# Which eighth of which channel a partition holds: s*16+k in the place of k*8+s

## The chip, the cores and the metric

The kernel runs on one core of a Trainium2 chip. A core has five engines that work side by side: TensorE (PE, with its weight loads as PEld), VectorE (DVE), ScalarE (ACT), GpSimd (POOL) and SyncE (SP), and 16 DMA engines that carry data between the memory of the chip (HBM) and the core's own memory (SBUF, 128 partitions). SP, ACT and POOL issue the transfers; each has its own queue. The metric is the device time of one execution in microseconds.

## The reference

The input x has 4 x 8 x 16 = 512 channels of 256 x 256 float32 values (256 KB each, 134 MB in all). Each channel is normalized by itself and scaled by its gamma:

```python
mu = x.mean(axis=(3, 4), keepdims=True)
var = ((x - mu) ** 2).mean(axis=(3, 4), keepdims=True)
x_norm = (x - mu) / np.sqrt(var + 1e-5)
out = x_norm * gamma[None, :, :, None, None]
```

Every value is read once and written once: 268 MB of traffic for two sums, one subtraction and one product a value.

## The kernel before, in words

The channels are worked in 32 units (U) of 16 channels (K). A channel is cut into S = 8 pieces of F = 8192 values (32 KB), so that the 16 x 8 = 128 pieces of a unit fill a tile of 128 partitions, 4 MB. In the kernel before, the view xv reads a unit as (p f): partition p holds the p-th 32 KB of the unit, so partition k*8+s holds piece s of channel k, and a unit is one unbroken stretch of HBM. The view ov does the same for the output.

There are AHEAD = 6 tiles (slots xt0 to xt5), each used in place for load, arithmetic and store. Six loads (line 48) are issued at the start, units 1 and 3 on ACT's queue and the others on SP's. Behind its two loads ACT gets 60 nops. POOL first issues two small transfers: a "touch" of the output with zeros (line 54, 16 rows of 512 B, later overwritten) and the load of gamma into one row (line 55). Then POOL makes constants, among them the matrix navg (lines 66 to 75): a memset to -1/65536 and two affine_selects that put zeros wherever the row and the column belong to different channels. As the partitions of one channel lie side by side, it is a matrix of 8x8 blocks on the diagonal. The gamma row is copied (line 83) into g_rep with 8 copies of each value, and 8 small matmuls turn that into g_col, one column of gammas a partition for each of the NG = 8 groups of channels.

The loop over units then does, for each:

- DVE sums each partition (line 107), while ACT sums its squares (line 108); both go to st.
- PE multiplies st by navg (line 116): each partition gets the sums of its whole channel, negated and divided by the number of values, as ps.
- DVE forms the negated variance (line 117), ACT its root (line 121), DVE the reciprocal (line 125) and the product with gamma (line 127).
- DVE applies mean and scale to the tile in place (line 130).
- ACT issues the store (line 134); SP issues the load of unit u+6 into the same slot, which waits for that store to end.

The order of the instructions on each engine is the program's own (a manual schedule); the queues are worked in order, SP's with loads and ACT's with stores behind its own arithmetic.

Of the kernel before, what the change touches and what calls it, by code (L numbers as in the profile page):

```python
# [1 line left out]

# [4 lines left out]

F32 = mybir.dt.float32
U8 = mybir.dt.uint8
ALU = mybir.AluOpType  # L10
ACTF = mybir.ActivationFunctionType
AX = mybir.AxisListType


@with_exitstack
def kernel(
    ctx: ExitStack,
    tc: tile.TileContext,
    x: bass.AP,
    gamma: bass.AP,  # L20
    out: bass.AP,
):
    nc = tc.nc
    B, G, C, H, W = x.shape
    P = nc.NUM_PARTITIONS
    HW = H * W
    n_ch = B * G * C
    S = 8
    K = P // S
    F = HW // S  # L30
    U = n_ch // K
    NG = (G * C) // K
    AHEAD = 6
    assert HW % S == 0 and (G * C) % K == 0

    xv = x.rearrange("b g c h w -> (b g c h w)").rearrange("(u p f) -> u p f", p=P, f=F)
    ov = out.rearrange("b g c h w -> (b g c h w)").rearrange("(u p f) -> u p f", p=P, f=F)
    gv = gamma.rearrange("g c -> (g c)")

    data = ctx.enter_context(tc.tile_pool(name="data", bufs=1))  # L40
    singles = ctx.enter_context(tc.tile_pool(name="singles", bufs=1))
    psum = ctx.enter_context(tc.tile_pool(name="psum", bufs=4, space=bass.MemoryType.PSUM))
    ctx.enter_context(tc.manual_schedule())

    slots = [data.tile([P, F], F32, name=f"xt{i}") for i in range(AHEAD)]

    def load(u, queue):
        queue.dma_start(out=slots[u % AHEAD][:], in_=xv[u])  # L48


    g_row = singles.tile([1, G * C], F32, name="g_row")
    touch = singles.tile([16, 128], F32, name="touch")
    nc.vector.memset(touch[:], 0.0)  # L53
    nc.gpsimd.dma_start(out=ov[0][0::S, 0:128], in_=touch[:])  # L54
    nc.gpsimd.dma_start(out=g_row[:], in_=gv[None, :])  # L55
    for u in range(AHEAD):
        load(u, nc.scalar if u in (1, 3) else nc.sync)

    for _ in range(60):
        nc.scalar.nop()  # L60

    eps_t = singles.tile([P, 1], F32, name="eps_t")
    nc.gpsimd.memset(eps_t[:], 1e-5)
    one = singles.tile([1, 1], F32, name="one")
    nc.gpsimd.memset(one[:], 1.0)
    navg = singles.tile([P, K, S], F32, name="navg")
    nc.gpsimd.memset(navg[:], -1.0 / HW)  # L67
    nc.gpsimd.affine_select(  # L68
        out=navg[:], in_=navg[:], pattern=[[-S, K], [0, S]], compare_op=ALU.is_ge,
        fill=0.0, base=0, channel_multiplier=1,  # L70
    )
    nc.gpsimd.affine_select(  # L72
        out=navg[:], in_=navg[:], pattern=[[S, K], [0, S]], compare_op=ALU.is_ge,
        fill=0.0, base=S - 1, channel_multiplier=-1,
    )
    navg_w = navg[:].rearrange("p k s -> p (k s)")
    root_eps = singles.tile([P, 1], F32, name="root_eps")
    nc.scalar.activation(out=root_eps[:], in_=eps_t[:], func=ACTF.Sqrt)  # L78
    g_rep = singles.tile([1, NG, K, S], F32, name="g_rep")
    g_ps = psum.tile([P, NG], F32, name="g_ps", bufs=1)  # L80
    g_col = singles.tile([P, NG], F32, name="g_col")

    nc.vector.tensor_copy(  # L83
        out=g_rep[:],
        in_=g_row[:].rearrange("o (n k) -> o n k", n=NG).unsqueeze(3).to_broadcast([1, NG, K, S]),
    )
    for n in range(NG):
        nc.tensor.matmul(  # L88
            out=g_ps[:, n : n + 1],
            lhsT=g_rep[:, n].rearrange("o k s -> o (k s)"),  # L90
            rhs=one[:],
            start=True, stop=True,
        )
    nc.vector.tensor_copy(out=g_col[:], in_=g_ps[:])  # L94

    junk = singles.tile([P, F], U8, name="junk")

    st = singles.tile([P, U, 2], F32, name="st")
    nvar = singles.tile([P, U], F32, name="nvar")
    std = singles.tile([P, U], F32, name="std")  # L100
    rstd = singles.tile([P, U], F32, name="rstd")
    scale = singles.tile([P, U], F32, name="scale")

    squares = []
    for u in range(U):
        t = slots[u % AHEAD]
        nc.vector.reduce_sum(out=st[:, u, 0:1], in_=t[:], axis=AX.X)  # L107
        square = nc.scalar.activation(  # L108
            out=junk[:], in_=t[:], func=ACTF.Square, accum_out=st[:, u, 1:2],
        )  # L110
        if u:

            tc.declare_no_dep(square.ins, squares[-1].ins, reason="junk, ordered by the root between")
        squares.append(square)
        ps = psum.tile([P, 2], F32, name="ps")
        nc.tensor.matmul(out=ps[:], lhsT=navg_w, rhs=st[:, u], start=True, stop=True)  # L116
        nc.vector.tensor_scalar(  # L117
            out=nvar[:, u : u + 1], in0=ps[:, 0:1], scalar1=ps[:, 0:1],
            scalar2=ps[:, 1:2], op0=ALU.mult, op1=ALU.add,
        )  # L120
        nc.scalar.activation(  # L121
            out=std[:, u : u + 1], in_=nvar[:, u : u + 1], func=ACTF.Sqrt,
            bias=eps_t[:], scale=-1.0,
        )
        nc.vector.reciprocal(out=rstd[:, u : u + 1], in_=std[:, u : u + 1])  # L125
        g = u % NG
        nc.vector.tensor_mul(  # L127
            out=scale[:, u : u + 1], in0=rstd[:, u : u + 1], in1=g_col[:, g : g + 1],
        )
        nc.vector.tensor_scalar(  # L130
            out=t[:], in0=t[:], scalar1=ps[:, 0:1], scalar2=scale[:, u : u + 1],
            op0=ALU.add, op1=ALU.mult,
        )
        nc.scalar.dma_start(out=ov[u], in_=t[:])
        if u + AHEAD < U:
            load(u + AHEAD, nc.sync)


# [1 line left out]
_INS = ['x', 'gamma']  # L140
_OUTS = [((4, 8, 16, 256, 256), 'float32')]


# [23 lines left out]
```

## Time and profile before

| What | Value |
|---|---|
| median of 3 runs | 626.86 us (626.76 to 626.90) |
| span of the profiled execution | 624.9 us (the page gives no other time of it) |
| bytes moved | 268.46 MB, 430 GB/s over the span |
| DVE busy | 443.4 us (71%) |
| ACT busy | 238.8 us (38%) |
| PE busy | 21.4 us (3%) |
| POOL busy | 2.4 us |
| sum of a tile (line 107, DVE) | 8.69 us, 32 times |
| squares of a tile (line 108, ACT) | 7.03 us, 32 times |
| scaling of a tile (line 130, DVE) | 4.55 us, 32 times |
| store, issue to landing | median 62.5 us |
| load on SP, issue to landing | median 38.5 us |

A profile page shows one execution. Its slices cut the span in 40 equal parts: the DMA digits are tenths of the 16 DMA engines' time, and GB/s is what they moved. A DMA queue is listed with its packets, bytes and share of 16 engines' time: q1 is SP's, q10 ACT's, q0 POOL's. The chain follows the last instruction back to what released it, step by step. A wait names the waiting engine, its line and what ended the wait. A window gives the busy time of every engine in one stretch of the span.

### The profile page before, as it was taken

What the parts mean: (1) busy time and instruction counts of PE and PEld (TensorE: products, weight loads), DVE (VectorE), ACT (ScalarE), POOL (GpSimd) and SP (SyncE); (2) the same over time, 40 slices, a digit from 0 to 9 for tenths busy, and PEclk for the clock granted to TensorE, in tenths of its full rate; (3) what the DMA queues carried; (4) which work ended last, traced back from release to release, by engine and by line L of the source; (5) the groups of instructions that cost most, each with busy time, mean ns of one, the idle gap of its engine ahead of it and who ended that gap; (6) DMA issues with size and microseconds to landing.
All of it is one profiled execution on the core that took longest, in us unless ns stands there. A gap on an engine that the chain in (4) does not pass through costs nothing.

```text
span 624.9 us, 631 instructions
## 1 busy us (share of the span) xinstructions
PE 21.4 (3%) x80; PEld 19.5 (3%) x80; DVE 443.4 (71%) x163; ACT 238.8 (38%) x98; POOL 2.4 (0%) x11
## 2 busy tenths in 40 slices
PE   0200000000000000000000000000000000000000
PEld 0200000000000000000000000000000000000000
DVE  0588999999776687666786767867668676687730
ACT  0444444444443234432344423444224442244400
POOL 1000000000000000000000000000000000000000
DMA  8999999999999999999999999999999999999998
GB/s 370 436 426 430 422 434 436 436 436 437 432 424 433 436 436 424 436 436 434 436 436 432 422 436 436 434 426 436 436 434 436 436 434 419 436 436 434 426 436 369
DMA packets 9282, 268.46 MB, mean 430 GB/s; under 512 B 1072, under 2 KB 1088, under 8 KB 1088
## 3 DMA queue, kind: packets, MB, share of 16 engines
q10 hardware_dynamic: 4896, 142.61, 52.9%
q1 hardware_dynamic: 4320, 125.83, 46.8%
q0 software_dynamic: 64, 0.01, 0.0%
q14 instruction: 2, 0.02, 0.0%
HBM read 134.22 MB, written 134.23 MB: 430 GB/s over the span
## 4 chain that ended last, share of the span: by engine, by line
another core or an unknown queue 61%; DMA 17%; DVE 15%; SPq 1%; PE 1%; issue 0%; ACT 0%
DVE st L107 10%; DMA xt<-in_x_dram 10%; DMA out_dram<-xt 8%; DVE xt L130 5%; SPq L48 1%; PE ps L116 1%; ACT std L121 0%; DVE nvar L117 0%; DVE rstd L125 0%; DVE scale L127 0%
## 5 line engine op out<-in xcount | busy, mean ns | idle before, releaser
L107 DVE TENSOR_REDUCE st<-xt 128x1 f32<-128x8192 f32 x32 | 277.9, 8685 | 100.4 <-DMA xt<-in_x_dram 100.4
L108 ACT ACTIVATE junk<-xt 128x8192 uint8<-128x8192 f32 x32 | 225.0, 7030 | 275.1 <-DMA xt<-in_x_dram 231.9
L130 DVE TENSOR_SCALAR xt<-xt,ps,scale 128x8192 f32<-128x8192 f32 x32 | 145.6, 4550 | 1.2
L121 ACT ACTIVATE std<-nvar,eps_t 128x1 f32<-128x1 f32 x32 | 9.4, 294 | 79.6 <-DVE nvar L117 79.6
L116 PE MATMUL ps<-st,navg 128*128 128x2 f32 x64 | 17.9, 349 | 557.1 <-DVE st L107 557.1
L116 PEld LDWEIGHTS ps<-st,navg 128*128 128x128 f32 x64 | 16.0, 311 | 558.9 <-issue 558.9
L117 DVE TENSOR_SCALAR nvar<-ps 128x1 f32<-128x1 f32 x32 | 9.2, 287 | 23.8 <-PE ps L116 23.8
L125 DVE RECIPROCAL rstd<-std 128x1 f32<-128x1 f32 x32 | 5.2, 164 | 11.6 <-ACT std L121 11.6
L83 DVE COPY g_rep<-g_row 1x1024 f32<-1x1024 f32 x1 | 0.7, 681 | 14.3 <-DMA g_row<-in_gamma_dram 14.3
L108 ACT ACTIVATION_READ_ACCUMULATOR junk<-xt 128x1 f32 x32 | 6.0, 186 | 0.0
L127 DVE TENSOR_TENSOR scale<-rstd,g_col 128x1 f32<-128x1 f32 x32 | 5.1, 159 | 1.1
L88 PE MATMUL g_ps<-one,g_rep 1*128 1x1 f32 x16 | 3.5, 347 | 16.1 <-DVE g_rep L83 16.1
L88 PEld LDWEIGHTS g_ps<-one,g_rep 1*128 1x128 f32 x16 | 3.5, 325 | 16.1 <-issue 16.1
L94 DVE COPY g_col<-g_ps 128x8 f32<-128x8 f32 x1 | 0.2, 166 | 3.7 <-PE g_ps L88 3.7
L78 ACT ACT_TABLE_LOAD x1 | 1.3, 1283 | 1.7 <-PEq L151 1.7
L53 DVE MEMSET touch<- 16x128 f32 x1 | 0.2, 165 | 0.9 <-PEq L151 0.9
L54 POOL DMA_DIRECT2D out_dram<-touch x1 | 0.6, 619 | 0.8 <-DVE touch L53 0.8
L55 POOL DMA_DIRECT2D g_row<-in_gamma_dram x1 | 0.5, 487 | 0.0
L68 POOL TENSOR_SCALAR_AFFINE_SELECT navg<-navg 128x128 f32<-128x128 f32 x1 | 0.4, 400 | 0.1
L72 POOL TENSOR_SCALAR_AFFINE_SELECT navg<-navg 128x128 f32<-128x128 f32 x1 | 0.4, 399 | 0.1
L67 POOL MEMSET navg<- 128x128 f32 x1 | 0.2, 232 | 0.0
L78 ACT ACTIVATE root_eps<-eps_t 128x1 f32<-128x1 f32 x1 | 0.2, 203 | 0.0
(6 smaller groups left out, 0.6 us busy)
## 6 DMA issues: line engine op xcount, KB each, us to landing
out_dram<-xt ACTq DMA_DIRECT2D x32, 4096.0 KB, 62.5
xt<-in_x_dram SPq DMA_DIRECT2D x30, 4096.0 KB, 38.5
xt<-in_x_dram ACTq DMA_DIRECT2D x2, 4096.0 KB, 31.5
out_dram<-touch POOLq DMA_DIRECT2D x1, 8.0 KB, 9.1
g_row<-in_gamma_dram POOLq DMA_DIRECT2D x1, 0.5 KB, 13.3
```

The lines of the kernel that those rows point to most:

```text
L48: queue.dma_start(out=slots[u % AHEAD][:], in_=xv[u])
L78: nc.scalar.activation(out=root_eps[:], in_=eps_t[:], func=ACTF.Sqrt)
L83: nc.vector.tensor_copy(out=g_rep[:], in_=g_row[:].rearrange("o (n k) -> o n k", n=NG).unsqueeze(3).to_broadcast([1, NG, K, S]),)
L88: nc.tensor.matmul(out=g_ps[:, n : n + 1], lhsT=g_rep[:, n].rearrange("o k s -> o (k s)"), rhs=one[:], start=True, stop=True,)
L107: nc.vector.reduce_sum(out=st[:, u, 0:1], in_=t[:], axis=AX.X)
L108: square = nc.scalar.activation(out=junk[:], in_=t[:], func=ACTF.Square, accum_out=st[:, u, 1:2],)
L116: nc.tensor.matmul(out=ps[:], lhsT=navg_w, rhs=st[:, u], start=True, stop=True)
L117: nc.vector.tensor_scalar(out=nvar[:, u : u + 1], in0=ps[:, 0:1], scalar1=ps[:, 0:1], scalar2=ps[:, 1:2], op0=ALU.mult, op1=ALU.add,)
L121: nc.scalar.activation(out=std[:, u : u + 1], in_=nvar[:, u : u + 1], func=ACTF.Sqrt, bias=eps_t[:], scale=-1.0,)
L125: nc.vector.reciprocal(out=rstd[:, u : u + 1], in_=std[:, u : u + 1])
L127: nc.vector.tensor_mul(out=scale[:, u : u + 1], in0=rstd[:, u : u + 1], in1=g_col[:, g : g + 1],)
L130: nc.vector.tensor_scalar(out=t[:], in0=t[:], scalar1=ps[:, 0:1], scalar2=scale[:, u : u + 1], op0=ALU.add, op1=ALU.mult,)
```

## The change

The views xv and ov cut a unit as (k s f) and walk it as s, then k, then f: partition s*16+k now holds piece s of channel k. In HBM, neighbouring partitions lie 256 KB apart, and each is a row of 32 KB. The number of transfers, their bytes and the queues that issue them are the same. What follows from the new order of partitions is changed with it: the averaging matrix has its non-zero values where row and column differ by a multiple of 16, and is made by a memset to 0 and 15 affine_selects, one for each such diagonal; g_rep repeats the 16 gammas of a group 8 times as a whole instead of each of them 8 times. The touch names the same bytes by the new view. The 60 nops on ACT are gone.

```diff
-    xv = x.rearrange("b g c h w -> (b g c h w)").rearrange("(u p f) -> u p f", p=P, f=F)
-    ov = out.rearrange("b g c h w -> (b g c h w)").rearrange("(u p f) -> u p f", p=P, f=F)
+    xv = x.rearrange("b g c h w -> (b g c h w)").rearrange("(u k s f) -> u s k f", k=K, s=S, f=F)
+    ov = out.rearrange("b g c h w -> (b g c h w)").rearrange("(u k s f) -> u s k f", k=K, s=S, f=F)
...
-    nc.gpsimd.dma_start(out=ov[0][0::S, 0:128], in_=touch[:])
+    nc.gpsimd.dma_start(out=ov[0][0, :, 0:128], in_=touch[:])
...
-    for _ in range(60):
-        nc.scalar.nop()
...
-    navg = singles.tile([P, K, S], F32, name="navg")
-    nc.gpsimd.memset(navg[:], -1.0 / HW)
-    nc.gpsimd.affine_select(
-        out=navg[:], in_=navg[:], pattern=[[-S, K], [0, S]], compare_op=ALU.is_ge,
-        fill=0.0, base=0, channel_multiplier=1,
-    )
-    nc.gpsimd.affine_select(
-        out=navg[:], in_=navg[:], pattern=[[S, K], [0, S]], compare_op=ALU.is_ge,
-        fill=0.0, base=S - 1, channel_multiplier=-1,
-    )
-    navg_w = navg[:].rearrange("p k s -> p (k s)")
+    navg_w = singles.tile([P, P], F32, name="navg")
+    nc.gpsimd.memset(navg_w[:], 0.0)
+    for m in range(-(S - 1), S):
+        nc.gpsimd.affine_select(
+            out=navg_w[:], in_=navg_w[:], pattern=[[-1, P]], compare_op=ALU.not_equal,
+            fill=-1.0 / HW, base=-m * K, channel_multiplier=1,
+        )
+    navg_w = navg_w[:]
...
-    g_rep = singles.tile([1, NG, K, S], F32, name="g_rep")
+    g_rep = singles.tile([1, NG, S, K], F32, name="g_rep")
...
-        in_=g_row[:].rearrange("o (n k) -> o n k", n=NG).unsqueeze(3).to_broadcast([1, NG, K, S]),
+        in_=g_row[:].rearrange("o (n k) -> o n k", n=NG).unsqueeze(2).to_broadcast([1, NG, S, K]),
...
-            lhsT=g_rep[:, n].rearrange("o k s -> o (k s)"),
+            lhsT=g_rep[:, n].rearrange("o s k -> o (s k)"),
```

## The prediction

> **What bounds the kernel now.** I read the page's slices first, then its DMA part, then the chain, then what the SP queue waits for, and last the windows of single stretches. The slices and the queues:
>
> ```profile
> DMA  8999999999999999999999999999999999999998
> GB/s 370 436 426 430 422 434 436 436 436 437 432 424 433 436 436 424 436 436 434 436 436 432 422 436 436 434 426 436 436 434 436 436 434 419 436 436 434 426 436 369
> DMA packets 9282, 268.46 MB, mean 430 GB/s; under 512 B 1072, under 2 KB 1088, under 8 KB 1088
> ...
> q10 hardware_dynamic: 4896, 142.61, 52.9%
> q1 hardware_dynamic: 4320, 125.83, 46.8%
> q0 software_dynamic: 64, 0.01, 0.0%
> ```
>
> The 16 DMA engines are full from the first slice to the last, while DVE is busy for 71% of the span and ACT for 38%. q1 carries SP's 30 loads, so one load is 4320 / 30 = 144 packets: 128 rows of 32 KB and 16 small closing ones. q10 carries ACT's 2 loads and 32 stores: 4896 / 34 = 144 again. So each 4 MB transfer is dealt out in 16 shares of 8 rows, each with one closing packet. q0 fits: the touch of 16 rows and the gamma row are 64 packets, 2 x (16 pieces + 16 closing ones).
>
> The SP queue's waits (us in total, times, longest) say that 26 of its loads wait for a store to leave their slot, not for arithmetic; the chain agrees, since its largest share is queue time between SP's issues, about 19 us at each:
>
> ```profile
> SPq L48 <- DMA out_dram<-xt: 534.4, 26, 59.5
> ```
>
> ```profile
> another core or an unknown queue 61%; DMA 17%; DVE 15%; SPq 1%; PE 1%; issue 0%; ACT 0%
> ...
> 178.96 0.33 SPq L48
> 179.29 18.95 another core or an unknown queue
> 198.30 0.33 SPq L48
> ```
>
> The pace of one engine comes out of the windows (columns: busy time of PE, PEld, DVE, ACT, POOL, PE clock, DMA share, GB/s; a packet is booked where it starts):
>
> ```profile
> 1.80:2.00 0.20, 0.00 (x0) 0.00 (x0) 0.00 (x0) 0.20 (x1) 0.20 (x2) 1.00 4.96 1475
> 10.00:15.00 5.00, 0.00 (x0) 0.00 (x0) 0.00 (x0) 0.00 (x0) 0.00 (x0) 1.00 1.00 433
> 22.60:600.30 577.70, 17.86 (x64) 16.04 (x64) 442.36 (x160) 237.34 (x96) 0.00 (x0) 1.00 1.00 433
> 616.40:618.80 2.40, 0.00 (x0) 0.00 (x0) 0.00 (x0) 0.00 (x0) 0.00 (x0) 1.00 1.01 437
> 617.20:617.40 0.20, 0.00 (x0) 0.00 (x0) 0.00 (x0) 0.00 (x0) 0.00 (x0) 1.00 0.38 164
> ```
>
> Row five holds one packet: 0.2 us at 164 GB/s is 32.8 KB, and 0.38 x 16 engines x 0.2 us is 1.22 us for it. Row three gives the same: 16 x 32.77 KB / 433 GB/s = 1.211 us. Loads alone (row two), loads and stores together (row three) and stores alone (row four) all run at 433 to 437, though they touch memory quite differently: an engine moves a row in 1.211 us (27.06 GB/s), whatever the row is. Row one, the first nine packets, shows a row at its slowest: 4.96 x 16 x 0.2 / 9 = 1.76 us, while everything starts.
>
> So the sum of the time before is 8192 rows / 16 engines x 1.211 = 620.0 us, and 4.9 us at the two ends make the page's span of 624.9. The page prints no other time of that execution; the median of the three runs, 626.86, stands 1.96 us (0.3%) above its span, and I add that at the end.
>
> **The change, part by part.** *The views xv and ov.* The old HBM side of a transfer was 128 rows of 32 KB, outermost count 128. The new one is 8 x 16 rows: 8 pieces outermost, 16 channels under each, and the two can't be merged into one stride because pieces are 32 KB apart and channels 256 KB. The tile's side stays 128 partitions. The number of rows, their size and the bytes are as before; what changes is how a transfer can be dealt to engines. SP's issue takes 0.33 us for 128 rows:
>
> ```profile
> 0.80 546.25 SPq L48 DMA_DIRECT2D xt<-in_x_dram  x30
> ```
>
> It carries two views, not a list of rows, so the dealing must be a rule on their counts. The forms in the trace are 128 rows (16 shares of 8) and 16 rows (16 shares of 1): both fit a cut of the outermost count into at most 16 equal shares. By that rule an outermost count of 8 gives 8 shares: 8 engines get 16 rows each, 8 get none. The other reading that fits the trace is that the rows are dealt out as one flat run of 128; then there are still 16 shares. No transfer of before has an outermost count under 16, so the trace does not decide. I take 8, because a cut of one count is the simpler rule and needs no merging of strides that do not merge. [...]
>
> The sum by 8 engines: 8192 / 8 = 1024 rows each x 1.211 = 1240.1 us. The ends stay: before, no row starts in the first 1.8 us, the first rows run at up to 1.76 us, and no row starts in the last 2.3 us (a window of 0 GB/s from 622.6); none of this grows with the number of rows, and I keep the 4.9. So 1245.0 of span, and 1.96 around it: 1247.0 us. Bounds of a row: not under 1.211, since three mixes of traffic share that floor, so the new order in memory brings no gain; not over 1.76 if every row met memory as the first ones did, which would be 1024 x 1.76 + 6.9 = 1809. I take 1.211, the value of 577 us against that of a fraction of one, and keep 1809 as a bound.
>
> *Does anything else come to the end of the path?* A period (one load, one store) is 19.35 us on the chain; it becomes 256 rows / 8 x 1.211 = 38.8 us. DVE needs 8.69 + 4.55 us for the two passes and 1.7 us of small steps, 15 us per tile, and ACT less, so the six slots feed the queues with still more to spare: one slot is in arithmetic for 15 of 38.8 us, the other five wait in queues. At the end, 3 stores are queued while the last tile is computed (585.3 to 600.3); three stores take 58 us then, against 15, so the tail stays covered.
>
> *The averaging matrix.* Two affine_selects of 0.40 us become 15, over the same 128x128:
>
> ```profile
> L68 POOL TENSOR_SCALAR_AFFINE_SELECT navg<-navg 128x128 f32<-128x128 f32 x1 | 0.4, 400 | 0.1
> L72 POOL TENSOR_SCALAR_AFFINE_SELECT navg<-navg 128x128 f32<-128x128 f32 x1 | 0.4, 399 | 0.1
> ```
>
> They start 0.47 apart in the timeline (2.82, 3.29), so POOL ends at 2.82 + 15 x 0.47 = 9.9 us instead of 3.7. The comparison is another (not_equal, not in the trace); at three times the cost, it would be 24 us. Its reader is the first weight load of L116, at 31.4 us before and, since loads 0 and 1 share the engines and land after 256 / 16 x 1.211 + 3.2 = 22.6 us now, after 256 / 8 x 1.211 + 3.2 = 42 us then, at about 51 after the change. Cost nothing; without that cover it would be 6.2 us once. POOL's two DMAs stand ahead of it in its order and are not moved.
>
> *The nops.* Sixty are taken from ACT behind its two load issues. ACT's issues end at 1.68, its table load begins at 1.72 and the next work is at 22.6, so gone or not they lie in 19 us of idle time: nothing. *The gamma row and its copy.* The same 1x1024 copy (0.68 us) and 16 matmuls (3.5 us) in another order; they end at 19.9, ahead of the first reduction at 22.6 on the same in-order DVE. The row lands at 15.3; if it waited behind everything until the first load at 42 us, 4.6 us would be added once at most. *The touch.* Row 0 of each channel, 16 rows 256 KB apart, before and after: the same bytes.
>
> **The rivals.** *Two engines on one path, slower still.* With 8 shares, an engine serves 16 neighbouring partitions and all walk them in step. If two of them meet at the same entrance of the tile's memory, a row of each takes 2 x 1.211. In lockstep throughout, that is 1024 x 2.422 + 6.9 = 2487 us; each tenth of the rows that meet adds 124 us, so it decides the time from the first tenth on. For it: an even start keeps engines in step, and nothing parts them. Against it: loads and stores alternate, so a pair half a period apart need not meet, and half of the engines are idle; in the trace of before, no stretch runs under the pace of 1.211 after the start. The trace can't show it, since each share of before is another set of partitions. [...]
>
> *Sixteen shares stay (not slower).* If the dealing flattens 8 x 16 into 128 rows, each engine has 8 rows of 1.211 and the time is 626.9. It decides by one number, the count of packets per transfer: 144 means this rival, 136 mine. A better order in memory could then gain at most the 22.6 x (1 - 395 / 433) = 2.0 us lost while the first loads run (395 GB/s up to 22.6 us), 0.3%; a worse one, with one row in fifty at 1.76 us, would cost 512 / 50 x 0.55 = 5.6 us. That the change does nothing it says is this case too.
>
> *Memory slows rows in the new order,* eight engines reading neighbouring pieces of one channel. For it: the first rows at 1.76. Against it: 433 GB/s for three mixes, and half the demand. Between 1247 and 1809; halfway 1528.
>
> **How the numbers follow.** Eight shares at the bare pace: 0.52, own range 1240 (the rows alone, without any ends) to 1275 (one row in twenty at 1.76 us: 51 x 0.55 = 28 us more). Pairs that meet: 0.30, from 1300 to 2487. Slow memory: 0.06. Sixteen shares: 0.12, of it 0.07 within 0.2% (about what this kernel's measurement can tell from no change; its three runs lie within 0.02%), 0.02 faster and 0.03 slower. So slower is 0.52 + 0.30 + 0.06 + 0.03 = 0.91. The predicted time is the likeliest case's 1247; the range takes in the pairs and slow memory, 1240 to 2490, and leaves out the 0.12.
>
> **What would show it.** After: 30 loads on q1 in 4080 packets, 4624 on q10, queue shares summing to about 50% of 16 engines, slices of about 216 GB/s, DVE at 36%, first reduction at about 42 us. One packet's window tells mine from the pairs: 0.38 share (1.22 us) or up to 0.76. POOL busy about 7.6 us, ended by 10. The prediction is wrong if q1 still has 4320 packets, or if slices lie near 110 GB/s.

## The result and the profile after

The changed kernel takes 1410.8 us (median of 6 runs, 1400.6 to 1434.9), the kernel before 627.0 us beside it: 2.244 times as long, with a 95% interval of 2.241 to 2.248; this ratio leaves out two runs that are some 2% longer than the other four, and the profiled execution is one of these two (1434.93 us, span 1433.1). The runs scatter by 2.5%, those of before by 0.1%; the section on the prediction comes back to that.

The page of the changed kernel, slices and queues:

```profile
DMA  4454544454455544555545454554554555455543
GB/s 103 102 110 102 124 177 206 202 205 202 202 198 201 209 207 203 203 205 203 204 204 210 207 201 203 205 205 202 207 209 205 205 205 207 201 204 199 134 169 142
DMA packets 8770, 268.46 MB, mean 187 GB/s; under 512 B 560, under 2 KB 576, under 8 KB 576
...
q10 hardware_dynamic: 4624, 142.61, 26.6%
q1 hardware_dynamic: 4080, 125.83, 23.1%
```

The bytes are the same, but a load is now 4080 / 30 = 136 packets: 128 rows and 8 closing ones, where it had 16. The queues' shares add up to 50% of 16 engines, which fits 8 that work all the time and 8 that don't work at all. That alone would give 216.5 GB/s (8 x 27.06). The GB/s row shows three stages: 102 to 110 at the start, 198 to 210 for most of the span, and a ragged end.

The same stages as windows of the changed kernel (columns as in the windows of before; the last two are the DMA share and GB/s):

```profile
0.00:160.00 160.00, 4.66 (x20) 4.49 (x20) 28.62 (x13) 16.32 (x8) 5.97 (x24) 1.00 0.50 105
160.00:1326.00 1166.00, 16.19 (x58) 14.54 (x58) 401.50 (x145) 215.09 (x87) 0.00 (x0) 1.00 0.50 202
1326.00:1433.10 107.10, 0.56 (x2) 0.50 (x2) 13.85 (x5) 7.42 (x3) 0.00 (x0) 1.00 0.44 149
```

At the bare pace of 8 engines the bytes of these three stages would take 160 x 105 / 216.5 = 78, 1166 x 202 / 216.5 = 1088 and 107 x 149 / 216.5 = 74 us, 1240 in all. So 82 us are lost in the first stage, 78 in the middle and 33 at the end: 193, which is all of 1433.1 - 1240.1. The DMA share of 0.50 in the first stage says that the 8 engines were not idle there: each row took twice its time (the packet records of this trace list 2.51 us on average, and never under 2.36, for the 472 rows that start between 10 and 158 us). At the end the share is 0.44, so by this share about 107 x 0.06 / 0.50 = 13 of the 33 us are engines that have run out of rows, and the other 20 are slow rows. This is the account of one long run; the median run takes 24 us less, and no trace shows in which stage.

What ends the first stage is on the timeline of the changed kernel (start, duration, instruction, idle time before it):

```profile
80.81 8.69 DVE L103 TENSOR_REDUCE st<-xt 128x1 f32<-128x8192 f32 x1 [50.47 <-DMA xt<-in_x_dram]
...
95.87 0.66 ACTq L130 DMA_DIRECT2D out_dram<-xt  x1
...
110.80 0.64 ACTq L130 DMA_DIRECT2D out_dram<-xt  x1
...
160.86 8.69 DVE L103 TENSOR_REDUCE st<-xt 128x1 f32<-128x8192 f32 x1 [50.09 <-DMA xt<-in_x_dram]
```

The first two tiles land at 80.8 and their stores are issued at 95.9 and 110.8, but ACT's queue still holds the load of unit 3 ahead of these stores. Unit 2 lands at 160.9, and until then all traffic goes one way: the packet records show 256 rows on ACT's queue, those of its two loads, up to 160 us, and the next one, the first of a store, at 167.0. From there on loads and stores run together, which is called mixed below. The end is one-way as well: the last load lands at 1326.0, and stores alone remain.

### The profile page after: what moved, and what is told of

Its sections match the earlier page's. It is cut to its first block, busy times and chain, and to the rows that moved or that the text cites. A ratio compares the mean times of both kernels' runs of the same rounds, so it can differ in the third digit from the quotient of the medians.

```text
span 1433.1 us, 658 instructions
## 1 busy us (share of the span) xinstructions
PE 21.4 (1%) x80; PEld 19.5 (1%) x80; DVE 444.0 (31%) x163; ACT 238.8 (17%) x98; POOL 6.0 (0%) x24
## 3 DMA queue, kind: packets, MB, share of 16 engines
q10 hardware_dynamic: 4624, 142.61, 26.6%
q1 hardware_dynamic: 4080, 125.83, 23.1%
## 4 chain that ended last, share of the span: by engine, by line
another core or an unknown queue 58%; DVE 31%; DMA 2%; PE 2%; ACT 1%; issue 1%; POOL 0%
DVE st L103 19%; DVE xt L126 10%; DMA g_row<-in_gamma_dram 2%; PE ps L112 1%; ACT std L117 1%; DVE nvar L113 1%; DVE rstd L121 0%; DVE scale L123 0%; PE g_ps L84 0%; DVE g_rep L79 0%; POOL out_dram L55 0%; DVE touch L54 0%; DVE g_col L90 0%
## 5 line engine op out<-in xcount | busy, mean ns | idle before, releaser
L113 DVE TENSOR_SCALAR nvar<-ps 128x1 f32<-128x1 f32 x32 | 9.2, 288 | 23.8 <-PE ps L112 23.8
L68 POOL TENSOR_SCALAR_AFFINE_SELECT navg<-navg 128x128 f32<-128x128 f32 x15 | 4.4, 292 | 1.0
## 6 DMA issues: line engine op xcount, KB each, us to landing
g_row<-in_gamma_dram POOLq DMA_DIRECT2D x1, 0.5 KB, 23.8
```

Of the source, the lines that this page charges most:

```text
L68: nc.gpsimd.affine_select(out=navg_w[:], in_=navg_w[:], pattern=[[-1, P]], compare_op=ALU.not_equal, fill=-1.0 / HW, base=-m * K, channel_ ...
L113: nc.vector.tensor_scalar(out=nvar[:, u : u + 1], in0=ps[:, 0:1], scalar1=ps[:, 0:1], scalar2=ps[:, 1:2], op0=ALU.mult, op1=ALU.add,)
```

## The experiments

The theory that I set out to test, called A in what was expected: the outermost count of the HBM view sets the number of shares, and two shares whose partitions lie 32 apart meet whenever they are in step and move data the same way. To meet means here that a row of each takes 2 x 1.211 us, as if both went through one entrance of the tile's memory; an entrance is a picture for it, and what traces can show is the pace. Theory A was an assumption until the runs below. Its rivals: rows far apart in memory are slow (B); fewer shares and nothing else (C); a slow start (G).

**Three other counts.** The first three kernels keep the form of the change with 16, 4 and 2 as the outermost count; the averaging matrix and the gammas follow, so that the result stays the normalized input. All three have the 60 nops of the kernel before.

```diff
-    xv = x.rearrange("b g c h w -> (b g c h w)").rearrange("(u p f) -> u p f", p=P, f=F)
+    xv = x.rearrange("b g c h w -> (b g c h w)").rearrange("(u b a f) -> u a b f", a=4, b=P // 4, f=F)
```

(ov likewise; a=16 and a=2 in the other two.)

> The same kind of walk with 16 as the outermost count: partition a*8+b takes the row b*16+a of its unit (16 rows 32 KB apart, under each of them 8 rows that lie 512 KB apart); the averaging matrix and the gammas follow. Theory A (the outermost count sets the shares, and shares whose partitions lie 32 apart meet at one entrance when they move the same way): 144 packets a transfer, so 4320 on SP's queue; shares a and a+4 meet, so the first stage, with loads alone, runs at about half of 433 GB/s (some 210), the mixed stage at 0.94 of 433 (some 406), and the time is about half of the changed kernel's: 700 us, 680 to 730. Theory B (rows far apart in memory slow each row, whatever the shares): rows at about 1.4 us everywhere, in the first stage no worse than later, 720 or more. Theory C (shares are all that matters, no meeting): 433 GB/s and 627 us.

> The same kind of walk with 4 as the outermost count: partition a*32+b takes the row b*4+a. Theory A: 4 shares of 32 rows, 132 packets a transfer, so 3960 on SP's queue; shares 0 and 1 meet, and 2 and 3, so loads alone run at about 52 GB/s (4 x 27.06 / 2), the mixed stage at about 102; about twice the changed kernel's time, 2820 us (2700 to 2900). Theory C (no meeting): 108 GB/s from the start, 2487 us.

> The same kind of walk with 2 as the outermost count: partition a*64+b takes the row b*2+a. Theory A: 2 shares of 64 rows, 130 packets a transfer, so 3900 on SP's queue; the two shares lie 64 apart and have entrances of their own, so they never meet: 54 GB/s with loads alone and 54 in the mixed stage, every row 1.21 us, 4096 x 1.211 + 7 = 4967 us. Its loads alone would thus run as fast as those of 4 shares. Theory D (shares slow each other for another reason, such as both walking memory in step): loads alone clearly under 54 GB/s.

Measured, with the changed kernel between them:

| Outermost count | Packets on SP's queue | Loads alone, GB/s | Mixed, GB/s | of engines x 27.06 | Time, us |
|---|---|---|---|---|---|
| 16 (walk16) | 4320 | 205 | 354 | 0.82 | 807.4 (785.8 to 822.6) |
| 8 (changed kernel) | 4080 | 105 | 204 | 0.94 | 1410.8 |
| 4 (walk4) | 3960 | 60 | 105 | 0.97 | 2698.1 |
| 2 (walk2) | 3900 | 54 | 54 | 1.00 | 4962.0 |

The windows behind it, first of walk16, then of walk4, then of walk2:

```profile
10.00:80.00 70.00, 4.66 (x20) 4.49 (x20) 28.53 (x13) 14.83 (x6) 0.00 (x0) 1.00 0.99 205
100.00:720.00 620.00, 15.05 (x54) 13.52 (x54) 365.64 (x135) 197.22 (x81) 0.00 (x0) 1.00 1.00 354
```

```profile
10.00:140.00 130.00, 3.54 (x16) 3.48 (x16) 1.05 (x5) 0.00 (x0) 3.25 (x5) 1.00 0.25 60
400.00:2400.00 2000.00, 13.97 (x50) 12.54 (x50) 346.17 (x125) 185.42 (x75) 0.00 (x0) 1.00 0.25 105
```

```profile
10.00:140.00 130.00, 3.54 (x16) 3.48 (x16) 0.92 (x3) 0.00 (x0) 0.00 (x0) 1.00 0.13 54
400.00:4500.00 4100.00, 15.84 (x54) 13.53 (x54) 367.85 (x135) 200.25 (x81) 0.00 (x0) 1.00 0.13 54
```

The packets are 30 x (128 + 16, 8, 4, 2): the outermost count is the number of shares in all four. The two shares of walk2 lie 64 partitions apart and never slow each other: 54 GB/s in both stages, and 4962 us against the 4967 worked out at 1.211 us a row. With four, loads alone run hardly faster than with two, though twice as many engines are at work. Theories C and D fall. Theory A missed twice: walk4 came out 4% under its 2820 and just below its range (its loads alone run at 60 GB/s where 52 was expected), and walk16 was 15% over its 700: its first stage was as forecast, the mixed one at 354 and not 406 GB/s. B had said 720 or more for walk16, so rows 512 KB apart were next to be ruled in or out.

**Distance in memory, with the shares kept.** Two kernels in which every share's rows follow each other in memory, so that only distance is gone: near8 with 8 shares, near16 with 16. The gap between shares stops the two outer counts from being one.

```diff
-    ... .rearrange("(u p f) -> u p f", p=P, f=F)
+    ... .rearrange("(v a w r f) -> v w a r f", a=8, w=2, r=16, f=F)
```

(a=16, r=8 in near16; loads and stores take xv[u // 2, u % 2]; the gammas follow.)

> Eight shares as in the changed kernel, but each share reads and writes 16 rows that follow each other in memory (512 KB in one piece); a tile takes every other such piece of 8 MB, so that the two outer counts cannot be merged. Partitions of a channel lie side by side as before the change. Theory A: memory has no part in it; 136 packets a transfer, 105 GB/s in the first 160 us, about 203 after, 1395 to 1440 us. Theory B (rows 256 KB apart are slow): rows of 1.21 us from the start, 216 GB/s, 1247 us. Theory E (what counts is only that partitions of one channel are 16 apart): 627 us.

> Sixteen shares of 8 neighbouring partitions, as in walk16, but each share's 8 rows follow each other in memory (one channel, 256 KB in one piece; a tile takes every other channel of 8 MB). It asks where walk16 lost the 100 us by which it was over its forecast. Theory F (shares that meet are all of it, and 16 shares come apart less well than 8): as walk16, 786 to 823 us, loads in the mixed stage at about 1.6 us a row. Theory B16 (with 16 shares the rows 512 KB apart are slow loads on top of the meeting): first stage at 206 GB/s as there, but the mixed stage at about 400 GB/s and 690 to 730 us.

near8 took 1409.3 us (1406.9 to 1415.0), 2.248 times the kernel before (2.242 to 2.254): the changed kernel's 2.244 with none of its distance. near16 took 804.6 us (801.1 to 809.9), within walk16's range of 785.8 to 822.6. Windows of near8, then of near16:

```profile
10.00:130.00 120.00, 4.65 (x20) 4.48 (x20) 28.93 (x19) 14.83 (x6) 0.00 (x0) 1.00 0.50 113
200.00:1280.00 1080.00, 15.06 (x54) 13.52 (x54) 365.72 (x135) 193.13 (x79) 0.00 (x0) 1.00 0.50 205
```

```profile
10.00:80.00 70.00, 4.66 (x20) 4.49 (x20) 28.93 (x19) 14.83 (x6) 0.00 (x0) 1.00 1.00 211
100.00:720.00 620.00, 15.06 (x54) 13.52 (x54) 376.05 (x136) 203.27 (x82) 0.00 (x0) 1.00 1.00 363
```

Both stages are close to those of the kernels with distance (113 for 105 and 205 for 204 GB/s, 211 for 205 and 363 for 354). B falls for 8 shares and B16 for 16: what walk16 lost beyond its forecast, it loses without any distance in memory too. Theory E, which wanted 627 us of near8, falls as well: there the partitions of a channel lie side by side, and it is as slow.

walk16 and near16 have 16 shares of 8 rows, and so has the kernel before, which loads at 433 GB/s where they load at 205 and 211. What differs must then be which rows a share takes, 8 neighbours in the one case and some other set of 8 in the other. No view of the trace names the partitions of a share, so this is inferred and not seen.

**Distance alone.** The reverse: 128 as the one outer count, as before the change, but rows 256 KB apart.

```diff
+    ... .rearrange("(v p w f) -> v w p f", p=P, w=8, f=F)
```

> One count of 128 as before the change, but with rows 256 KB apart: a tile takes one piece of each of 128 channels. The sums over 8 neighbouring partitions then run over 8 channels and not over one, so what is normalized is not what the reference normalizes; instructions, bytes and order of work are those of before. It is the distance in memory alone. Theory A: 144 packets, 1.211 us a row, 627 us (625 to 632). Theory B (distance slows rows): over 640, with rows over 1.211 us in the middle of the span.

It took 627.35 us (ratio 1.0008, interval 0.9999 to 1.0017), at 432 GB/s in the middle of the span:

```profile
30.00:560.00 530.00, 16.76 (x60) 15.05 (x60) 405.37 (x150) 215.43 (x89) 0.00 (x0) 1.00 1.00 432
```

So rows 256 KB apart cost nothing that can be measured. What costs is that the transfer is two counts with 8 outermost (1409.3 us in near8, without that distance). The order s*16+k itself can't be written as one count, since pieces lie 32 KB apart and channels 256 KB; far128 is another order.

**The rest of the change.** No nops, and the 15 affine_selects made on top of the old matrix, on a spare one.

```diff
-    for _ in range(60):
-        nc.scalar.nop()
+    spare = singles.tile([P, P], F32, name="spare")
+    nc.gpsimd.memset(spare[:], 0.0)
+    for m in range(-(S - 1), S):
+        nc.gpsimd.affine_select(out=spare[:], in_=spare[:], pattern=[[-1, P]], ...)
```

> All of the change but its views: the kernel before without the 60 nops, and with the 15 affine_selects made as well, into a spare matrix ahead of the one that is used. All theories: POOL works to about 11 us, the first weight load of the averaging is at 31 us; 626.9 us, within 0.2%.

626.84 us, ratio 0.9999 (0.9990 to 1.0008): nothing, as expected. The new order of the gamma copy and the new form of the touch are not in this kernel; near8 has neither of them, and the matrix of before, and yet the changed kernel's time.

**Direction.** The changed kernel with all first loads on SP's queue, so that no load stands ahead of the first store.

```diff
-        load(u, nc.scalar if u in (1, 3) else nc.sync)
+        load(u, nc.sync)
```

> The changed kernel with all six first loads on SP's queue, so that the first stores do not stand behind unit 3's load on ACT's queue. Theory A with direction (pairs meet only while all traffic goes the same way): loads alone last until the first store, at about 60 us and not 165, the pace then goes to about 203 GB/s; 100 us at 105 GB/s fewer are worth 100 x (1 - 105/203) = 48 us: 1362, 1340 to 1380. Theory G (the slow first 165 us are a start that takes its time whatever the traffic): as the changed kernel, 1400 to 1435.

It took 1370.0 us (1355.9 to 1391.4), ratio 2.185 (2.175 to 2.195) against 2.244. The first store is issued at 57.5, and the pace leaves 105 GB/s there, a hundred microseconds earlier than in the changed kernel. Windows of this run:

```profile
20.00:50.00 30.00, 2.35 (x12) 2.26 (x11) 7.70 (x2) 7.12 (x2) 0.00 (x0) 1.00 0.49 105
...
60.00:70.00 10.00, 0.00 (x0) 0.00 (x0) 0.00 (x0) 0.00 (x0) 0.00 (x0) 1.00 0.50 144
70.00:80.00 10.00, 0.00 (x0) 0.00 (x0) 0.00 (x0) 0.00 (x0) 0.00 (x0) 1.00 0.49 197
80.00:100.00 20.00, 0.56 (x2) 0.50 (x2) 13.85 (x5) 7.42 (x3) 0.00 (x0) 1.00 0.51 216
```

From 105 to 216 within some 40 us of the first store: theory A with direction holds, and G falls. That two queues are at work is not enough, since in the first 160 us of the changed kernel both SP's and ACT's queue carry loads (232 and 240 rows between 10 and 158 us), at 105. Nor does the pace stay up for good: in this run it is back at 120 GB/s between 270 and 290 us.

**Which partitions meet.** Seven transfers in two shares each, one after the other, ahead of the kernel before: (1) to (4) load partitions 0 to 31, 0 to 63, 32 to 95 and 0 to 127, (5) and (6) store partitions 0 to 63 and 32 to 95, and (7) is a store and a load of partitions 0 to 63 side by side.

```diff
+    a, c = slots[0], slots[1]
+    nc.sync.dma_start(out=a[0:32], in_=rows(x, 32))
+    nc.sync.dma_start(out=a[0:64], in_=rows(x, 64))
+    nc.sync.dma_start(out=a[32:96], in_=rows(x, 64))
+    nc.sync.dma_start(out=a[:], in_=rows(x, 128))
+    nc.scalar.dma_start(out=rows(out, 64), in_=a[0:64])
...
+    nc.scalar.dma_start(out=rows(out, 64), in_=a[32:96])
...
+    nc.scalar.dma_start(out=rows(out, 64), in_=a[0:64])
+    nc.sync.dma_start(out=c[0:64], in_=rows(x, 64))
```

(rows(t, n) is the first n rows of t in the form "(b a f) -> a b f" with a=2; three one-column memsets on DVE keep the stores apart. The kernel behind them has all its first loads on SP's queue.)

> The kernel before, with seven transfers put ahead of its loads, one after the other, each dealt in two shares (outermost count 2), so that it can be read which partitions meet. A row alone takes 1.211 us. [...] Some 420 us (one to 80 more for (7)) ahead of the 627. Theory H (any two shares slow each other, or it is the memory side): (2) and (3) take the same time.

Windows inside each of the transfers (2) to (7), of this run:

```profile
30.00:90.00 60.00, 0.00 (x0) 0.00 (x0) 0.00 (x0) 0.00 (x0) 0.00 (x0) 1.00 0.12 27
105.00:140.00 35.00, 0.00 (x0) 0.00 (x0) 0.00 (x0) 0.00 (x0) 0.00 (x0) 1.00 0.13 54
150.00:210.00 60.00, 0.00 (x0) 0.00 (x0) 0.00 (x0) 0.00 (x0) 0.00 (x0) 1.00 0.13 55
230.00:270.00 40.00, 0.00 (x0) 0.00 (x0) 0.00 (x0) 0.00 (x0) 0.00 (x0) 1.00 0.12 30
300.00:330.00 30.00, 0.00 (x0) 0.00 (x0) 0.00 (x0) 0.00 (x0) 0.00 (x0) 1.00 0.12 52
...
360.00:400.00 40.00, 0.00 (x0) 0.00 (x0) 0.00 (x0) 0.00 (x0) 0.00 (x0) 1.00 0.13 54
341.00:360.00 19.00, 0.00 (x0) 0.00 (x0) 0.00 (x0) 0.00 (x0) 0.00 (x0) 1.00 0.12 43
```

and what SP waited for, before its transfers (2), (3) and (4), of this run (us, times, longest):

```profile
SPq L64 <- DMA xt<-in_x_dram: 78.0, 1, 78.0
...
SPq L65 <- DMA xt<-in_x_dram: 40.8, 1, 40.8
SPq L63 <- DMA xt<-in_x_dram: 21.4, 1, 21.4
```

Line 63 waits for (1), 32 rows in two shares 16 partitions apart: 21.4 us, near the 19.4 of 16 rows at 1.211, so they don't meet. Line 64 waits for transfer (2), partitions 0 to 63: 78.0 us at 27 GB/s, the pace of one engine, though the share of 0.12 says that two are busy; that is 2.44 us for each of a share's 32 rows. Line 65 waits for (3), the same 64 rows of HBM on partitions 32 to 95: 40.8 us at 54 GB/s. The shares lie 32 apart in both, so it is not distance in the tile but which partitions: 0-31 and 32-63 meet (27 GB/s), 32-63 and 64-95 do not (54), and neither do 0-63 and 64-127 in (4) (55). Stores meet like loads, a little less hard: (5) 30, (6) 52 GB/s. And (7), a load and a store on the very partitions that meet, begins slowly (43 GB/s until 360) and then runs at 54 with a share of 0.13, which is two engines at the bare pace: as if one share loaded while the other stored, in turns, though no view names the rows of a share. Theory H falls.

The seven transfers end at about 420 us (SP issues the next load at 419.6), as expected. That sum has the rows of (2) and (5) at twice 1.211 us, an estimate that no earlier run showed for these partitions; the two took 78.0 and 69.7 us. The single run took 1086.2 us, some 40 more than 420 and 627 together; why the rest took longer is not known.

**Why 16 shares lose more.** Half of the data, on tiles of 64 partitions, in 8 shares of 8 rows (half8) and in 4 of 16 (half4), so that a share has as few rows as with twice the engines:

```diff
-    ... .rearrange("(u p f) -> u p f", p=P, f=F)
+    ... .rearrange("(v a w r f) -> v w a r f", a=8, w=2, r=8, f=F)
...
-        t = slots[u % AHEAD]
+        t = slots[u % AHEAD][0:64]
```

> Why do 16 shares keep only 354 to 363 of 433 GB/s in the mixed stage (0.82 to 0.84), 8 shares 204 of 216.5 (0.94), 4 shares 105 of 108 (0.97)? Tiles of 64 partitions in 8 shares of 8 rows; half of the data is left out (32 tiles of 2 MB, the other half of the output is not written, gammas as before). [...] Theory H (the number of engines at work, or the load on memory, does it): 0.94, about 204 GB/s (200 or more).

> [...] Theory H: that of 4 shares, 0.97 or better, 105 GB/s or more.

Each ran once, in 755.5 and 1379.2 us. Mixed stage of half8, then of half4:

```profile
100.00:680.00 580.00, 9.56 (x56) 7.97 (x56) 378.88 (x140) 203.67 (x84) 0.00 (x0) 1.00 0.50 195
```

```profile
200.00:1250.00 1050.00, 8.88 (x52) 7.39 (x52) 358.97 (x130) 192.83 (x78) 0.00 (x0) 1.00 0.25 104
```

195 of 216.5 is 0.90, under theory H's 0.94 and its range of 200 GB/s or more; 104 of 108 is 0.96, just under its 0.97. A share of half the rows loses a little more (0.94 to 0.90, and 0.97 to 0.96), but not what 16 shares lose (0.82). Whether that little is due to the shorter shares or to the smaller tiles and transfers isn't shown, since all halve together. Counted for one load and one store (their bytes at the measured pace, less the same at the bare pace), the changed kernel and walk4 lose 2.4 us each, half8 2.1 and half4 1.6, but walk16 4.3 and near16 3.7. Why 16 shares lose more stays open; the number of engines at work and the load on memory go together in these kernels.

## Why the prediction was right, and where it was not

The direction was right, and the time lies in the range of 1240 to 2490; the predicted 1247 us is 12% under the measured 1410.8, outside the likeliest case's own range of 1240 to 1275. The range, a factor of two wide, holds the time because it takes in a rival; the mechanism behind the 1247 was half right, in the 8 shares, and wrong in taking it that these shares don't slow each other.

- *The dealing into 8 shares* came true to the packet: 136 a load, 4080 and 4624 on the queues, 50% of 16 engines. The runs with 16, 4 and 2 shares confirm the cut of the outermost count; the reading as one flat run of 128 rows, rival "sixteen shares", is out. That a count of 8 gives 8 shares was my reading, which no trace of before could show; the 136 packets show it.
- *1024 rows at 1.211 us, and the ends as they were*: this is the step that failed. The sum gave 1240.1 + 4.9 of span; the profiled span is 1433.1. The row's own time was right (two shares keep it over the whole 4962 us), but I gave 52 chances in 100 to pairs that don't meet, and pairs do meet. The case that I gave 30 in 100, two engines on one path, is what happened, far from its price of 2487 us: lockstep throughout is true of the 160 us of loads alone and partly true of the last 107. At my price of 124 us for each tenth of the rows that meet, the 164 us over 1247 are 13% of the rows. One of my signs of being wrong, slices near 110 GB/s, came true for the first four of the 40 slices (102 to 110).
- *The argument against that rival* ("loads and stores alternate, so a pair half a period apart need not meet") was right where both directions run, and transfer (7) shows it (54 GB/s); the argument for it ("nothing parts them") was wrong there. What I did not look at was how long traffic goes one way. That sentence took it that the traffic is mixed from the start; ACT's queue has a load ahead of the first stores, and that made the one-way stage 160 us long instead of some 60. Taking it away was worth 41 us (1410.8 to 1370.0), against 48 worked out. Which shares pair up, no trace of before showed either; (2) against (3) shows it for partitions 0 to 95. That partitions above 64 pair up like those below is shown less directly: no transfer has them alone, but between 10 and 158 us of the changed kernel every row takes at least 2.36 us, so those of all 8 engines do.
- *Slow memory in the new order*: no part in it. near8 without distance has the changed kernel's time, far128 with distance alone has that of before.
- *The slots and the tail*: the 8 engines are full from the first load to 1410 us, as forecast, but then run out unevenly (a DMA share of 0.38 from 1410 to 1420, then 0.19, where 0.50 is full), which I had not. A period in the middle is 2 x 4.19 MB / 204 GB/s = 41 us, not 38.8, and the first reduction starts at 80.8, not 42: the first two loads alone pay the meeting in full.
- *The small edits* cost nothing, shown by no_views. In the changed kernel an affine_select takes 0.29 us, not the 0.40 taken from the old pair; the gamma row lands 23.8 us after its issue, not 13.3, and stays ahead of the first reduction.

The scatter of the changed kernel's runs fits the same cause, though this is argued and not shown: how soon a pair falls into turns, and how long the last stores stay in step, is not set by the program. The two runs of walk2, whose shares never meet, agree within 0.3 us of 4962.

## What to carry to other kernels

Before rewriting a view, look at its outermost count, not only at its strides: packets per transfer on the profile's queues told here how many engines share it: 144, 136, 132 and 130 for 128 rows in 16, 8, 4 and 2 shares, with a DMA share of 1.00, 0.50, 0.25 and 0.13. Choose an order of partitions whose 128 rows are one count (rows 256 KB apart were free that way, 627.35 us in far128); 16 outer by 8 inner still has all the engines and costs 28% (804.6 us in near16). If shares do meet, mixed traffic hides most of it (204 of 216.5 GB/s in the changed kernel) and one-way traffic next to nothing (105), so keep loads off the queue that carries the first stores (1370.0 against 1410.8 us).

## What the hardware showed that I had not expected

- Two shares that meet come to the full pace by themselves when each has loads and stores to do: 27 GB/s when all goes one way (transfer 2), 54 within 26 us of both directions being there (transfer 7, issued at 334.3, 54 from 360), 105 to 216 within some 40 us with eight (one_queue8). That they fall into turns is argued and not shown.
- All 16 engines can be busy all the time (DMA share 1.00) and move 354 GB/s instead of 433, because the time that a packet is listed as busy grows when shares meet: transfers (2) and (3) both show two busy engines (shares of 0.12 and 0.13), at 27 and 54 GB/s, and the packet records of the changed kernel list 2.51 us for a row between 10 and 158 us, against a median of 1.21 from 160 to 1326. A full DMA row in the slices doesn't mean full speed; GB/s beside it does.
- Shares that all go one way run a little above half the bare pace in some runs, as if they came apart by themselves: stores more than loads in transfers (5) and (2) (30 and 27 GB/s), loads too in walk4 and near8 (60 and 113 GB/s, where half the bare pace of 4 and 8 engines is 54 and 108); and the changed kernel's last stage, stores only, averages 149 GB/s where its first, loads only, keeps 105.
